# Channel shuffle in 32 equal tiles: small tiles at both ends, six buffers, copies shared by VectorE and ScalarE

## The chip, the cores and the metric

The kernel runs on one core of one Trainium2 chip. The metric is the device time of one execution in microseconds (us), lower is better. "Span" is the part of an execution that the profile's records cover; the time is 1.7 to 2.2 us longer than the span.

## The reference

```python
batch, h, w, c = 16, 64, 64, 256          # float32, groups = 8
x = x.reshape(batch, h, w, groups, channels_per_group)
x = x.transpose(0, 1, 2, 4, 3)            # swap group and channel in the group
x = x.reshape(batch, h, w, c)
```

It is a pure permutation inside each pixel of 256 channels. It computes nothing, reads 67.11 MB from HBM and writes 67.11 MB back.

## The kernel before

There are 32 tiles of 16 pixels a partition (2 MB each). A tile is loaded by SyncE's DMA queue, permuted by one copy within SBUF, on GpSimd for even tiles and on VectorE for odd ones, and stored by ScalarE's DMA queue. There are five buffers for loads and five for stores.

```python
_Q = int(os.environ.get("CS_Q", "16"))
_IN_BUFS = int(os.environ.get("CS_IN_BUFS", "5"))
_OUT_BUFS = int(os.environ.get("CS_OUT_BUFS", "5"))
_COPY_ENGINES = os.environ.get("CS_COPY_ENGINES", "gv")
# ... cut ...
    for t in range(ntiles):
        in_tile = in_pool.tile([P, free], mybir.dt.float32)
        nc.sync.dma_start(out=in_tile, in_=x_t[t])

        out_tile = out_pool.tile([P, free], mybir.dt.float32)

        src = in_tile.rearrange("p (i g j) -> p i j g", g=G, j=CPG)
        dst = out_tile.rearrange("p (i j g) -> p i j g", j=CPG, g=G)
        do_copy(copy_engines[t % len(copy_engines)], dst, src)

        nc.scalar.dma_start(out=out_t[t], in_=out_tile)
```

Of the kernel before, what the change touches and what calls it, by code (L numbers as in the profile page):

```python
# [2 lines left out]

# [4 lines left out]


_Q = int(os.environ.get("CS_Q", "16"))
_IN_BUFS = int(os.environ.get("CS_IN_BUFS", "5"))
_OUT_BUFS = int(os.environ.get("CS_OUT_BUFS", "5"))
_COPY_ENGINES = os.environ.get("CS_COPY_ENGINES", "gv")


@with_exitstack
def kernel(
    ctx: ExitStack,
    tc: tile.TileContext,  # L20
    x: bass.AP,
    groups: bass.AP,
    out: bass.AP,
):
    nc = tc.nc

    b, h, w, c = x.shape
    G = int(groups)
    CPG = c // G
    assert G * CPG == c, (c, G)  # L30

    P = nc.NUM_PARTITIONS

    n_pix = b * h * w
    assert n_pix % P == 0

    q = _Q
    pix_per_tile = P * q
    ntiles = n_pix // pix_per_tile
    assert ntiles * pix_per_tile == n_pix, (n_pix, pix_per_tile)  # L40

    free = q * c

    x_t = x.rearrange("b h w c -> (b h w c)").rearrange(
        "(t p f) -> t p f", p=P, f=free
    )
    out_t = out.rearrange("b h w c -> (b h w c)").rearrange(
        "(t p f) -> t p f", p=P, f=free
    )

    in_pool = ctx.enter_context(tc.tile_pool(name="in_pool", bufs=_IN_BUFS))
    out_pool = ctx.enter_context(tc.tile_pool(name="out_pool", bufs=_OUT_BUFS))

    eng_map = {"v": nc.vector, "g": nc.gpsimd, "s": nc.scalar}
    copy_engines = [eng_map[ch] for ch in _COPY_ENGINES]

    def do_copy(eng, dst, src):
        if eng is nc.scalar:
            eng.copy(out=dst, in_=src)
        else:  # L60
            eng.tensor_copy(out=dst, in_=src)  # L61

    for t in range(ntiles):
        in_tile = in_pool.tile([P, free], mybir.dt.float32)
        nc.sync.dma_start(out=in_tile, in_=x_t[t])  # L65

        out_tile = out_pool.tile([P, free], mybir.dt.float32)

        src = in_tile.rearrange("p (i g j) -> p i j g", g=G, j=CPG)
        dst = out_tile.rearrange("p (i j g) -> p i j g", j=CPG, g=G)  # L70
        do_copy(copy_engines[t % len(copy_engines)], dst, src)

        nc.scalar.dma_start(out=out_t[t], in_=out_tile)


# [1 line left out]
_INS = ['x', 'groups']  # L77
_OUTS = [((16, 64, 64, 256), 'float32')]
#: Inputs that are plain numbers.
_NUMBERS = {'groups': 8}  # L80


# [26 lines left out]
```

## Time and profile before

| | before |
|---|---|
| time, median (range) | 318.0 us (317.92 to 318.02) |
| span of the profiled execution | 316.3 us |
| DMA, mean over the span | 424 GB/s |
| GpSimd busy / VectorE busy | 36% / 20% |

From the profile's page: the share of time that the 16 DMA engines are busy, in 40 equal slices of the span (9 is 90% or more), what they moved in each slice, and the DMA queues (q1 and q10 carry the loads and the stores), with packets, MB and the time of their packets as a share of the 16 engines' span.

```profile
DMA  7999999999999999999999999999999999999997
GB/s 290 431 402 431 431 431 431 431 431 433 431 431 431 431 431 431 431 431 431 431 431 431 431 431 431 431 431 431 431 431 431 431 431 431 431 431 431 433 431 332
...
q1 hardware_dynamic: 4608, 67.11, 50.0%
q10 hardware_dynamic: 4608, 67.11, 49.5%
HBM read 67.11 MB, written 67.11 MB: 424 GB/s over the span
```

38 of 40 slices are at 90% or more, nearly all at 431 GB/s, and the packets of the two queues fill 99.5% of the engines' time. The copies are far from that. These are the groups of instructions: count, busy us, mean ns of one, then the idle time before them and what ended it.

```profile
L61 POOL COPY out_tile<-in_tile 128x4096 f32<-128x4096 f32 x16 | 114.5, 7157 | 182.3 <-DMA in_tile<-in_x_dram 182.3
L61 DVE COPY out_tile<-in_tile 128x4096 f32<-128x4096 f32 x16 | 63.8, 3985 | 240.0 <-DMA in_tile<-in_x_dram 240.0
```

Both engines that copy idle for most of the span, waiting for loads. Here are the busy time, DMA share and GB/s in some stretches (microseconds of the span, a packet is counted where it starts):

```profile
core 0: us, DVE busy (x) POOL busy (x), PEclk, DMA share, GB/s
2.00:4.00 2.00, 0.00 (x0) 0.00 (x0) 1.00 0.72 246
4.00:9.00 5.00, 0.00 (x0) 0.43 (x1) 1.00 1.00 426
...
30.00:290.00 260.00, 51.47 (x14) 92.44 (x13) 1.00 1.01 431
290.00:314.00 24.00, 3.89 (x1) 7.11 (x1) 1.00 1.00 430
314.00:315.00 1.00, 0.00 (x0) 0.00 (x0) 1.00 0.43 180
315.00:316.00 1.00, 0.00 (x0) 0.00 (x0) 1.00 0.00 0
...
```

The engines are full from 4 us on; 180 GB/s in the last microsecond with traffic, nothing after 315 us.

### The profile page before, as it was taken

Reading aid. Unit: us, or ns where it says so; the run is one execution under the profiler, and the core shown is the slowest. Engines: PE = TensorE matmul, PEld = TensorE weight load, DVE = VectorE, ACT = ScalarE, POOL = GpSimd, SP = SyncE. Lnnn points to the kernel's source line nnn. Section 1 sums busy time; section 2 is a strip of 40 time slices with the busy share of each in tenths; the row PEclk is TensorE's granted clock in tenths of the full one; section 3 lists DMA queues with packets and bytes.
Section 4 is the critical chain, followed back from the end, with each engine's and each line's share of the span. In section 5 each row is a group of like instructions: output and inputs, shape, how many; then the busy total and the mean of one; then the engine's idle time right before and its main releaser. Section 6 shows DMA issues by size and latency. Waiting matters only on the chain.

```text
span 316.3 us, 247 instructions
## 1 busy us (share of the span) xinstructions
DVE 63.8 (20%) x16; POOL 114.7 (36%) x20
## 2 busy tenths in 40 slices
DVE  0344004040130402204021040310404004040040
POOL 0863350803508044080530806217062260713500
DMA  7999999999999999999999999999999999999997
GB/s 290 431 402 431 431 431 431 431 431 433 431 431 431 431 431 431 431 431 431 431 431 431 431 431 431 431 431 431 431 431 431 431 431 431 431 431 431 433 431 332
DMA packets 9216, 134.22 MB, mean 424 GB/s; under 512 B 1024, under 2 KB 1024, under 8 KB 1024
## 3 DMA queue, kind: packets, MB, share of 16 engines
q1 hardware_dynamic: 4608, 67.11, 50.0%
q10 hardware_dynamic: 4608, 67.11, 49.5%
HBM read 67.11 MB, written 67.11 MB: 424 GB/s over the span
## 4 chain that ended last, share of the span: by engine, by line
DMA 94%; DVE 1%; SPq 0%; issue 0%; DVEq 0%
DMA in_tile<-in_x_dram 94%; DVE out_tile L61 1%; SPq L65 0%; DVEq L61 0%
## 5 line engine op out<-in xcount | busy, mean ns | idle before, releaser
L61 POOL COPY out_tile<-in_tile 128x4096 f32<-128x4096 f32 x16 | 114.5, 7157 | 182.3 <-DMA in_tile<-in_x_dram 182.3
L61 DVE COPY out_tile<-in_tile 128x4096 f32<-128x4096 f32 x16 | 63.8, 3985 | 240.0 <-DMA in_tile<-in_x_dram 240.0
L90 POOL MEMSET const-float32-0.0<- 128x1 f32 x1 | 0.1, 99 | 0.2 <-issue 0.2
L90 POOL MEMSET const-bfloat16-1.0<- 128x1 bf16 x1 | 0.1, 103 | 0.0
L90 POOL MEMSET const-uint8-127<- 128x1 uint8 x1 | 0.1, 103 | 0.0
L90 POOL MEMSET const-float32-1.0<- 128x1 f32 x1 | 0.1, 99 | 0.0
## 6 DMA issues: line engine op xcount, KB each, us to landing
in_tile<-in_x_dram SPq DMA_DIRECT2D x32, 2048.0 KB, 38.8
out_dram<-out_tile ACTq DMA_DIRECT2D x32, 2048.0 KB, 25.3
```

Source lines behind the costliest of these rows:

```text
L61: eng.tensor_copy(out=dst, in_=src)
L90: nc = _bacc.Bacc("TRN2", target_bir_lowering=False, num_devices=1)
```

## The change

The intent is to start storing earlier and to finish with a short tail: tiles of 4, 4 and 8 pixels a partition first and 8, 4, 4 last. Each copy is split in two halves, on VectorE and ScalarE, to shorten it, and there are six buffers instead of five. The diff, cut to its core:

```diff
-_Q = int(os.environ.get("CS_Q", "16"))
-_IN_BUFS = int(os.environ.get("CS_IN_BUFS", "5"))
-_OUT_BUFS = int(os.environ.get("CS_OUT_BUFS", "5"))
-_COPY_ENGINES = os.environ.get("CS_COPY_ENGINES", "gv")
+_SIZES = [4, 4, 8] + [16] * 30 + [8, 4, 4]
+_IN_BUFS = 6
+_OUT_BUFS = 6
+_SHARES = (("vector", 1), ("scalar", 1))
 # ... cut ...
-    for t in range(ntiles):
-        in_tile = in_pool.tile([P, free], mybir.dt.float32)
-        nc.sync.dma_start(out=in_tile, in_=x_t[t])
 # ... cut ...
-        do_copy(copy_engines[t % len(copy_engines)], dst, src)
-        nc.scalar.dma_start(out=out_t[t], in_=out_tile)
+    for q in _SIZES:
+        in_tile = in_pool.tile([P, biggest * c], F32, name="in_tile")
+        nc.sync.dma_start(out=in_tile[:, : q * c], in_=rows(x_flat, first, q))
+        out_tile = out_pool.tile([P, biggest * c], F32, name="out_tile")
+        at, total = 0, sum(n for _, n in _SHARES)
+        for k, (engine, n) in enumerate(_SHARES):
 # ... cut: upto = end of this engine's share of the q pixels ...
+                permute(engine, out_tile[:, cols], in_tile[:, cols])
+        nc.scalar.dma_start(out=rows(out_flat, first, q), in_=out_tile[:, : q * c])
+        first += P * q
```

More of the change, by code (lines that the diff above doesn't have):

```diff
@@ L2 @@
-import os
 from contextlib import ExitStack
@@ L8 @@
 from concourse._compat import with_exitstack
-_Q = int(os.environ.get("CS_Q", "16"))
-_IN_BUFS = int(os.environ.get("CS_IN_BUFS", "5"))
-_OUT_BUFS = int(os.environ.get("CS_OUT_BUFS", "5"))
-_COPY_ENGINES = os.environ.get("CS_COPY_ENGINES", "gv")
+F32 = mybir.dt.float32
+P = 128
+_SIZES = [4, 4, 8] + [16] * 30 + [8, 4, 4]
+_IN_BUFS = 6
+_OUT_BUFS = 6
+_SHARES = (("vector", 1), ("scalar", 1))
 @with_exitstack
@@ L29 @@
     CPG = c // G
-    assert G * CPG == c, (c, G)
-    P = nc.NUM_PARTITIONS
-    n_pix = b * h * w
-    assert n_pix % P == 0
-    q = _Q
-    pix_per_tile = P * q
-    ntiles = n_pix // pix_per_tile
-    assert ntiles * pix_per_tile == n_pix, (n_pix, pix_per_tile)
-    free = q * c
-    x_t = x.rearrange("b h w c -> (b h w c)").rearrange(
-        "(t p f) -> t p f", p=P, f=free
-    )
-    out_t = out.rearrange("b h w c -> (b h w c)").rearrange(
-        "(t p f) -> t p f", p=P, f=free
-    )
+    assert G * CPG == c
@@ L51 @@
+    assert sum(_SIZES) * P == b * h * w
+    biggest = max(_SIZES)
+    x_flat = x.rearrange("b h w c -> (b h w c)")
+    out_flat = out.rearrange("b h w c -> (b h w c)")
     in_pool = ctx.enter_context(tc.tile_pool(name="in_pool", bufs=_IN_BUFS))
     out_pool = ctx.enter_context(tc.tile_pool(name="out_pool", bufs=_OUT_BUFS))
-    eng_map = {"v": nc.vector, "g": nc.gpsimd, "s": nc.scalar}
-    copy_engines = [eng_map[ch] for ch in _COPY_ENGINES]
-    def do_copy(eng, dst, src):
-        if eng is nc.scalar:
-            eng.copy(out=dst, in_=src)
-        else:
-            eng.tensor_copy(out=dst, in_=src)
@@ L63, with rows @@
-    for t in range(ntiles):
-        in_tile = in_pool.tile([P, free], mybir.dt.float32)
-        nc.sync.dma_start(out=in_tile, in_=x_t[t])
-        out_tile = out_pool.tile([P, free], mybir.dt.float32)
-        src = in_tile.rearrange("p (i g j) -> p i j g", g=G, j=CPG)
-        dst = out_tile.rearrange("p (i j g) -> p i j g", j=CPG, g=G)
-        do_copy(copy_engines[t % len(copy_engines)], dst, src)
-        nc.scalar.dma_start(out=out_t[t], in_=out_tile)
+    def rows(flat, first, q):
+        return flat[first * c : (first + P * q) * c].rearrange("(p f) -> p f", p=P)
@@ new lines, in permute @@
+    def permute(engine, dst, src):
+        src = src.rearrange("p (i g j) -> p i j g", g=G, j=CPG)
+        dst = dst.rearrange("p (i j g) -> p i j g", j=CPG, g=G)
+        if engine == "scalar":
+            nc.scalar.copy(out=dst, in_=src)
+        else:
+            getattr(nc, engine).tensor_copy(out=dst, in_=src)
+    first = 0
+    for q in _SIZES:
[4 more added lines that the diff above has]
+        for k, (engine, n) in enumerate(_SHARES):
+            last = k == len(_SHARES) - 1
+            upto = q if last else min(q, at + -(-q * n // total))
+            if upto > at:
+                cols = slice(at * c, upto * c)
+                permute(engine, out_tile[:, cols], in_tile[:, cols])
+            at = upto
+        nc.scalar.dma_start(out=rows(out_flat, first, q), in_=out_tile[:, : q * c])
+        first += P * q
```

## The prediction

> **What bounds the kernel now.** The 16 DMA engines. The page's slices show a DMA share of 90% or more and 431 GB/s in nearly all 40 slices; the first (290 GB/s) and the last (332 GB/s) are clearly lower. The chain of waits gives 94% of the 316.3 us span to loads. VectorE is busy 20%, GpSimd 36%, and in the list of waits both wait only for loads (240.0 and 182.3 us). The Trainium skill, "DMA: Bandwidth & Descriptors", section "Where 436 GB/s comes from", gives 435 GB/s as the ceiling of the 16 ports; the trace agrees with 431 to 433 in steady slices.
>
> The chain repeats every 38.84 us for four tiles in and four out: 9.71 us a tile (2.1 MB each way), 432 GB/s. All 134.22 MB at this rate take 310.7 us. Small windows show the first packets at about 1.5 us and the last at 314.5 us. So only about 5.6 us of the span is not steady transfer: 1.5 before the first packet, about 2.3 in ramp-up and where stores begin (98 to 262 GB/s at 2.5 to 3.5 us, 246 GB/s at 19 us), 1.8 for the last store to be confirmed.
>
> **What the change does.**
> - Halved copies: today 7.1 us (GpSimd) or 3.9 us (VectorE) a tile. VectorE's half is about 1.95 us (half of 3.87). ScalarE's half, 2048 elements, is estimated at 1.9 us from the Trainium skill, "ScalarE: Activation LUTs", section "What ACT_TABLE_LOAD costs" (186 ns + 0.833 ns an element). No ScalarE copy is in this trace. Copies wait for loads, not the reverse: worth 0. A table load on ScalarE, if any, precedes the first landing: 0.
> - Six buffers instead of five: loads are in flight continuously already (SyncE's queue waits 244.1 us for loads, 3.2 for copies). Worth 0.
> - Small first tiles: the first store starts at about 7 us instead of 15.7. But loads fill the DMA engines from 3.5 us on, so an earlier store only displaces load packets. Worth 0. Issues of about 0.42 us still outpace a 0.5 MB tile (1.2 us).
> - Small last tiles: the last copy ends at 303.7 us with 10.6 us of stores still queued, so its latency is hidden already. After the change stores lag loads less (I estimate 3 to 4 MB, 7 to 9 us, instead of 6 MB), still more than receipt, half copy and issue (4 to 6 us). Worth 0.
> - Added: 4 loads, 4 stores, and packets of 4 and 8 KB instead of 16 KB in 12 transfers, some 0.1 to 0.5 us; ramp-up may change by half a microsecond either way.
>
> **Prediction.** Nearly nothing changes on the critical path: 318.2 us, range 317.4 to 319.1. Faster by over 2%: 0.01; within 2%: 0.97; slower: 0.02.
>
> **What would show the steps.** 431 GB/s throughout; GpSimd idle, ScalarE and VectorE near 65 us each; first store issued at 6 to 8 us; first packet near 1.5 us, last about 1.8 us before the end. From the last load's landing to the end shrinks from 16.6 us to 7 to 11 us without the span shrinking: the loads simply end later.
>
> **What would make it wrong.** A store queue that runs dry at the end, a visible gap of DMA share in the last slice (up to 4 us, 1%); small packets that slow the engines; ScalarE copies much longer than 2 us, delaying the stores it issues; or a steady rate that depends on how loads and stores interleave, which one trace can't show.

## The result, and the profile after

| | before | after |
|---|---|---|
| time, median (range) | 318.01 us (317.92 to 318.13) | 319.16 us (318.76 to 319.61) |
| span of the profiled execution | 316.3 us | 317.5 us |
| ratio (95% interval) | 1 | 1.0036 (1.0022 to 1.005) |

A ratio here is the mean time of one kernel's fast runs over that of the other's of the same rounds, so it is not quite the ratio of the medians that are quoted. Within 2% nothing changed, as predicted. But the change is slower by 1.15 us, and that is clear of noise; the measured 319.16 us lies 0.06 us above the predicted range. What was to be explained is one microsecond in 318.

The same parts of the page:

```profile
DMA  7999999999999999999999999999999999999996
GB/s 285 401 430 427 429 431 431 431 431 431 431 431 429 436 433 429 433 431 431 429 428 429 431 429 433 431 431 431 430 429 436 431 428 433 431 431 428 420 441 281
...
q1 hardware_dynamic: 5184, 67.11, 49.8%
q10 hardware_dynamic: 5184, 67.11, 49.5%
q14 instruction: 3, 0.02, 0.0%
HBM read 67.11 MB, written 67.11 MB: 423 GB/s over the span
```

The share is still 9 nearly everywhere and the rate still about 431. Two things differ. The last slice falls from 332 to 281 GB/s, and there is a new queue, q14, that carries instructions: three packets. The copies:

```profile
L49 ACT COPY out_tile<-in_tile 128x2048 f32<-128x2048 f32 x30 | 111.0, 3708 | 171.6 <-DMA in_tile<-in_x_dram 171.6
L51 DVE COPY out_tile<-in_tile 128x2048 f32<-128x2048 f32 x30 | 62.3, 2075 | 218.9 <-DMA in_tile<-in_x_dram 218.9
```

ScalarE takes 3.71 us for half a tile, not 1.9; VectorE takes 2.08. Both still wait only for loads, as the list of waits says (engine and line, what it waited for, us in total, times, longest):

```profile
DVE out_tile L51 <- DMA in_tile<-in_x_dram: 242.1, 36, 8.3
ACT out_tile L49 <- DMA in_tile<-in_x_dram: 188.0, 33, 13.8
```

The chain of waits gives loads 81% and stores 8%. ScalarE's copies get 3%, which are single links and not an accumulated cost:

```profile
DMA in_tile<-in_x_dram 81%; DMA out_dram<-out_tile 8%; ACT out_tile L49 3%; SPq L56 1%; ACTq L66 0%
```

The stretches show where the time went:

```profile
core 0: us, DVE busy (x) ACT busy (x) POOL busy (x), PEclk, DMA share, GB/s
2.00:4.00 2.00, 0.00 (x0) 0.01 (x1) 0.00 (x0) 1.00 0.93 369
4.00:9.00 5.00, 1.50 (x3) 2.43 (x3) 0.00 (x0) 1.00 1.01 369
...
30.00:290.00 260.00, 55.28 (x28) 98.11 (x28) 0.00 (x0) 1.00 1.01 431
290.00:314.00 24.00, 3.63 (x4) 7.72 (x4) 0.00 (x0) 1.00 1.00 424
314.00:315.00 1.00, 0.00 (x0) 0.00 (x0) 0.00 (x0) 1.00 0.87 356
315.00:316.00 1.00, 0.00 (x0) 0.00 (x0) 0.00 (x0) 1.00 0.23 94
316.00:317.00 1.00, 0.00 (x0) 0.00 (x0) 0.00 (x0) 1.00 0.03 12
```

From 30 to 290 us there is no visible difference. At 4 to 9 us, though, the change moves 369 GB/s where the kernel before moves 426. From 2 to 4 us it is the other way round (369 against 246), so that over 2 to 9 us both move nearly the same, 2.58 and 2.62 MB: the mean rate shows next to no loss at the start. At the end the engines no longer stop together: traffic trickles on at 94 and 12 GB/s from 315 us, when the kernel before has ended. When the mean rate falls from 356 to 94 GB/s in one microsecond, some of the 16 engines are done and others are not. So the question is not how busy the DMA engines are on average, but which of them ends last.

### One DMA engine at a time

The trace records each packet's start and duration, but not its engine. In the steady stretch that can be recovered: an engine starts a 16 KB packet every 607 ns, so the starts form 16 chains, one for each engine, and each has to carry 512 such packets' worth of bytes. Chains that start close to each other are easily confused, above all in the last 30 us of the change, where packets of 4, 8 and 16 KB mix. A second rule keeps them apart: on each queue, every transfer puts eight data packets of equal size and then one of 4 bytes on each engine (each queue has 576 packets of 4 bytes for the 36 transfers of the change). Following the chains from 35 us after the first packet to the end gives, for each engine, the end of its last packet and how much it had lost by 35 us against back-to-back packets. A slip is a packet that starts late against its chain. Times here count from the first packet (1.76 us of the span before, 1.77 after). The last five engines of each kernel, worked out in this way from the packet records:

```
                 before                         after
          end us   lost by 35 us        end us   lost by 35 us   slips after 35 us
last      313.35   2.20                 314.60   2.42            305 + 533 ns, at instruction packet 2
          313.14   1.99                 314.43   2.54            306 + 244 ns, at instruction packet 1
          313.02   1.87                 313.97   1.56            306 + 424 ns, at instruction packet 3
          313.02   1.86                 313.92   2.58            none
          313.01   1.85                 313.85   2.52            none
```

Not every packet can be given to one chain with certainty. Every assignment from 150 us on that was found to fit both rules well has the same two engines last. The third line is uncertain: another chain lies so close that the 424 ns, or this end, may be its own, and the line's numbers leave some 0.3 us of its end unexplained.

The last packet ends 1.25 us later (314.60 against 313.35), and the spans differ by 1.24 us. Of this, 0.84 us are the two slips beside the second instruction packet, and 0.22 us is what the last engine lost more in the first 35 us (2.42 against 2.20). The other 0.19 us came later: 0.56 us lost from 35 us to the end, without the slips, instead of 0.37, for the extra small packets and completions (4 KB packets start every 155 ns, a quarter of 607 would be 152). The average engine explains much less than that: the mean of all 16 ends is 0.46 us later. Five engines had lost 2.42 to 2.58 us by 35 us, the others at most 1.92. Two of the five also carried an instruction packet, and these two end last; two that carried none end 0.50 and 0.57 us after the last engine of the kernel before. So two costs met on the same engines here, and there they add.

In the first microseconds the mean number of DMA engines that are busy, in steps of 0.5 us of the span, from the same records (overlapping packets counted as 16 at most):

```
span us from       3.0   3.5   4.0   4.5   5.0   5.5   6.0   6.5   7.0   7.5
before            15.7  16.0  16.0  16.0  16.0  16.0  16.0  16.0  16.0  16.0
after             16.0  16.0  16.0  13.4  15.3  16.0  16.0  16.0  15.4  14.1
```

At 4.5 us, once the two first loads of 0.5 MB are through and the third load should follow, engines stand idle: 4 of the 16 at 4.8 us, and all are busy again at 5.3 us, so no engine loses more than about 0.6 us here. No store has begun at that time (the first packet of a store starts at 9.5 us). There is a second, shorter dip from 7.4 to 7.8 us. It is likely, but not shown, that the five engines which had lost most by 35 us are the ones that stood idle here.

Here are the DMA queues in the stretch from 158 to 161 us of the span, where one of the instruction packets falls:

```profile
q10 hardware_dynamic: 42, 0.69, 53.5%
q1 hardware_dynamic: 37, 0.61, 47.6%
q14 instruction: 1, 0.01, 0.6%
```

It takes 309 ns on one engine. The chain of that engine slips by 306 ns at this very point, and 0.85 us later by another 244 ns, for which the records have no packet. At the other two packets the slips are 305 and 533 ns, and 306 and 424 ns (the last one perhaps on another chain). The packets come about 3 to 5 us after the 64th recorded instruction of ScalarE, the 64th of VectorE, and the 79th of SyncE. The kernel before ends with 67 recorded instructions on ScalarE, 47 on VectorE and 71 on SyncE, and has no such packet in its span. The Trainium skill, "Runtime: NRT & Kernel Launch", section "Instruction fetch mechanics", says that a sequencer fetches the next block of its program over a DMA queue of its own while it executes the current one, in blocks of 16 KiB, and calls the cost "mostly hidden". The trace agrees so far that no wait of a compute engine is put down to these packets. But it shows a packet of 8 KB, and the DMA engine that carries it falls behind.

### The profile page after: what moved, and what is told of

It is laid out like the page before. It is cut to its first block, busy times and chain, and to the rows that moved or that the text cites. A ratio compares the mean times of both kernels' runs of the same rounds, so it can differ in the third digit from the quotient of the medians.

```text
span 317.5 us, 339 instructions
## 1 busy us (share of the span) xinstructions
DVE 67.2 (21%) x36; ACT 120.8 (38%) x37; POOL 0.2 (0%) x4
## 4 chain that ended last, share of the span: by engine, by line
DMA 88%; another core or an unknown queue 5%; ACT 3%; SPq 1%; issue 0%; ACTq 0%
DMA in_tile<-in_x_dram 81%; DMA out_dram<-out_tile 8%; ACT out_tile L49 3%; SPq L56 1%; ACTq L66 0%
## 5 line engine op out<-in xcount | busy, mean ns | idle before, releaser
L49 ACT COPY out_tile<-in_tile 128x2048 f32<-128x2048 f32 (+2 forms) x36 | 119.5, 3326 | 188.1 <-DMA in_tile<-in_x_dram 188.0
L51 DVE COPY out_tile<-in_tile 128x2048 f32<-128x2048 f32 (+2 forms) x36 | 67.2, 1868 | 242.1 <-DMA in_tile<-in_x_dram 242.1
```

Of the source, the lines that this page charges most:

```text
L49: nc.scalar.copy(out=dst, in_=src)
L51: getattr(nc, engine).tensor_copy(out=dst, in_=src)
```

## The experiments

My theory is this. The end is set by the slowest of 16 saturated DMA engines. The change loses on single engines, (1) at the small first loads, because the next load's packets are not there when a small one is through, and (2) at instruction packets, which come with more instructions.

The rivals are: (A) the halved copies or ScalarE's late issue of stores; (B) the small last tiles, which let the engines end apart; (C) instruction packets are harmless; (D) the early small stores disturb the loads.

All twelve runs gave correct results. "Span" is the median of a run's five executions; "last packet" and "after it" (the time from the last packet to the end of the span) are of the profiled one, and so is "beyond" (the time minus the span).

| run | time us (range) | ratio to before (95%) | span | last packet at | after it | beyond |
|---|---|---|---|---|---|---|
| before | 318.04 (317.93 to 318.37) | | 316.3 | 315.11 | 1.16 | 1.73 |
| the change | 319.16 (318.76 to 319.61) | 1.0036 (1.0022 to 1.005) | 317.4 | 316.37 | 1.14 | 1.79 |
| even tiles | 318.96 (318.67 to 319.11) | 1.0026 (1.0013 to 1.0039) | 317.2 | 315.53 | 1.66 | 1.77 |
| no small first | 319.08 (319.01 to 319.2) | 1.0031 (1.0019 to 1.0044) | 317.3 | 315.46 | 1.79 | 1.79 |
| no small last | 319.11 (318.92 to 319.64) | 1.0038 (1.0024 to 1.0051) | 317.3 | 315.97 | 1.37 | 1.77 |
| small tiles alone | 319.46 (318.97 to 319.98) | 1.0045 (1.0032 to 1.0058) | 317.3 | 315.88 | 1.37 | 2.19 |
| spare instructions | 318.52 (318.43 to 318.93) | 1.0018 (1.0005 to 1.003) | 316.7 | 315.54 | 1.16 | 1.77 |
| many spare instructions | 350.19 (348.03 to 350.58) | 1.1006 (1.0991 to 1.1021) | 348.4 | | | |
| small tiles, 2nd load on other queue | 318.70 (318.6 to 318.8) | 1.0019 (1.0007 to 1.0032) | 316.5 | 315.19 | 1.23 | 2.18 |
| small last alone | 318.63 (318.28 to 319.17) | 1.0017 (1.0005 to 1.003) | 316.6 | 315.57 | 1.43 | 2.17 |
| copies in quarters | 318.32 (318.14 to 318.51) | 1.0009 (0.9996 to 1.0021) | 316.5 | 315.58 | 1.17 | 1.76 |
| the change, 2nd load on other queue | 318.71 (318.65 to 318.86) | 1.0022 (1.001 to 1.0035) | 316.9 | 315.60 | 1.29 | 1.77 |
| six buffers alone | 318.12 (317.97 to 318.33) | 1.0004 (0.999 to 1.0018) | 316.3 | 315.02 | 1.16 | 1.79 |
| the change again | 318.96 (318.81 to 319.45) | 1.0034 (1.0021 to 1.0046) | 317.2 | 315.75 | 1.29 | 1.77 |

The row "before" takes its time from the nine executions beside the first four experiments, the rest from the profile before. Beside the other two groups of four it measured 318.04 and 318.08 us. The change's own ratio and its repetition are from two sessions. The first four experiments, the next four and the last four ran on three different chips, each group beside the kernel before.

From the packet records of the profiled executions, the engine that ended last in each run (us after the first packet; where chains could not be followed from 35 us, the loss is by a later time, which adds up to 0.1 us):

| run | last engine ends | lost by 35 us | slips at an instruction packet |
|---|---|---|---|
| before | 313.35 | 2.20 | |
| the change | 314.60 | 2.42 | 305 + 533 ns |
| even tiles | 313.81 | 1.82 | 306 + 531 ns |
| no small first | 313.74 | 1.57 | 306 + 531 ns |
| no small last | 314.24 | 3.08 | |
| small tiles alone | 314.15 | 2.82 | |
| small tiles, 2nd load on other queue | 313.42 | 2.20 (by 120 us) | |
| small last alone | 313.81 | 2.48 | |
| copies in quarters | 313.84 | 1.84 | 306 + 530 ns |
| the change, 2nd load on other queue | 313.87 | 1.70 (by 80 us) | 306 + 406 ns |
| six buffers alone | 313.26 | 2.11 | |
| the change again | 314.02 | 1.63 (by 50 us) | 306 + 409 ns |

Some loss at the start is always there, and it varies: without small first tiles the worst engine of one of these runs (not always the one that ended last) lost 2.07 to 2.48 us by 35 us, with them and one load queue 2.31 to 3.08 us.

### Undoing one part of the change (three runs) and doing the tiles alone (one run)

Even tiles:

```diff
-_SIZES = [4, 4, 8] + [16] * 30 + [8, 4, 4]
+_SIZES = [16] * 32
```

> The change with all 32 tiles of 16 pixels (halved copies and six buffers stay). Theory: the slowest of the 16 DMA engines sets the end; the change loses on single engines, about 1.0 to 1.4 us at the small first loads (load queue dry between small tiles) and about 0.6 to 0.8 us on one engine for each of three instruction-fetch packets that the trace shows in mid-run. So this run loses only the fetches: 318.4 to 318.8 us. Rival A, the halved copies and ScalarE's later issue of stores cost the time: as the changed kernel, 319.0 to 319.4. Rival B, the small last tiles cost it: as before, 318.0.

No small first tiles:

```diff
-_SIZES = [4, 4, 8] + [16] * 30 + [8, 4, 4]
+_SIZES = [16] * 31 + [8, 4, 4]
```

> The change without its small first tiles (31 tiles of 16, then 8, 4, 4). Theory: the loss at the first loads goes, the fetches and a little packet overhead (0.1 to 0.2 us) stay: 318.5 to 319.0 us. Rival B (small last tiles let the engines end apart): no gain, 319.0 to 319.4.

No small last tiles:

```diff
-_SIZES = [4, 4, 8] + [16] * 30 + [8, 4, 4]
+_SIZES = [4, 4, 8] + [16] * 31
```

> The change without its small last tiles (4, 4, 8, then 31 tiles of 16). Theory: the first loads still run dry, so 318.9 to 319.3 us, and the last slice is as ragged as with the whole change. Rival B: 318.0 to 318.4 us and all engines end together.

Small tiles alone, in the changed kernel's code:

```diff
-_IN_BUFS = 6
-_OUT_BUFS = 6
-_SHARES = (("vector", 1), ("scalar", 1))
+_IN_BUFS = 5
+_OUT_BUFS = 5
+_WHOLE = ("gpsimd", "vector")
 # in the loop, in place of the two halves:
+        permute(_WHOLE[t % 2], out_tile[:, : q * c], in_tile[:, : q * c])
```

> The kernel before (whole copies in turn on GpSimd and VectorE, five buffers) with the small tiles first and last. Theory: the loss at the first loads is there without halved copies: 318.6 to 319.2 us, fewer instruction-fetch packets in the span. Rival A (halved copies, ScalarE): 318.0 to 318.3 us.

Read by times alone these four say nothing sensible: small tiles alone cost all of the loss (+1.4 us), all the rest without small tiles costs most of it (+0.9), and taking away either end's small tiles wins nothing. The costs don't add over the runs. That is how a maximum over engines behaves: take away what delays the last engine, and the next one is nearly as late.

The traces tell them apart. Small tiles alone has no instruction packet in its span, and its four last engines (314.00 to 314.15 us after the first packet) are those that lost 2.67 to 2.82 us by 35 us, against 2.20 us at most before. Only 11.1 and 12.1 of 16 engines are busy at 4.5 and 5.0 us of the span. Even tiles is full there. Its last engine had lost only 1.82 us by 35 us, but it carried the second instruction packet (slips of 306 and 531 ns) and ended at 313.81. With no small last tiles, the last engine, at 314.24, lost 3.08 us by 35 us and carried no packet; those with the second and the third packet come next, at 313.73 and 313.70.

Rival A falls as the whole cause, since small tiles alone loses more without any ScalarE copy. But even tiles shows that the halved copies (with six buffers, which alone cost nothing, see below) do cost 0.9 us; in its trace the engine that ends last is one that carries an instruction packet, not one that waits for a late store. Rival B falls too: without small last tiles the loss is as large as with them. My numbers for even tiles (up to 318.8) and for small tiles alone (up to 319.2) were 0.2 and 0.3 us too low; no small first tiles (up to 319.0) came out 0.1 us too high for my range, inside the range that I had given to rival B. The last columns of the first table show what I had not counted. In even tiles the span ends 1.66 us after the last packet (1.14 to 1.43 in the runs with no packet there), and a third instruction packet falls in just that time; from 316 to 317.2 us the DMA queues hold nothing else:

```profile
q14 instruction: 1, 0.01, 2.4%
```

No small first tiles has 1.79 us there, also with a packet at 316.88 us. In the three runs whose "beyond" is 2.17 us or more, an instruction packet comes after the end of the span; in all the other runs there is none there, and "beyond" is 1.79 us at most. That looks like a cost of 0.2 to 0.6 us for a fetch at the very end. It is read from the traces' coincidence only; no run here changed it by itself.

### Instructions without any change of transfers (three runs)

```diff
+        for _ in range(2):                      # 14 in the second run
+            nc.vector.memset(spare[0], 0.0)
+            nc.gpsimd.memset(spare[1], 0.0)
         nc.scalar.dma_start(out=out_t[t], in_=out_tile)
```

> The kernel before with two tiny memsets a tile more on VectorE and on GpSimd (their results are never used); no transfer changes. In the traces so far a packet of 8 KB of the instruction queue appears in mid-run just after ScalarE's and VectorE's 64th recorded instruction, and the one DMA engine that carries it ends 0.55 to 0.85 us later than it would. Theory: VectorE (47 recorded instructions before) and GpSimd (56) now pass 64, so two instruction packets in mid-run, two DMA engines late, 318.2 to 318.9 us depending on which engines carry them. Rival C (the DMA engines end apart because of the copies' or the stores' timing, instruction packets are harmless): two packets, but 317.9 to 318.1 us as before.

> As the run before, with 14 spare memsets a tile on VectorE and on GpSimd, some 500 recorded instructions on each. Theory: about four instruction packets for each of the two, eight in all, some on the same DMA engine: 318.6 to 319.8 us. Rival C: 317.9 to 318.2 us.

The first gave 318.52 us, in the predicted range, but the test was not clean. The spare memsets depend on nothing, so all of them were placed at the start of both engines' programs, as the timeline shows (start, us, engine, line):

```profile
0.73 10.29 POOL L78 MEMSET spare<- 128x8 f32 x64 [0.29 <-POOLq L97]
0.81 8.46 DVE L77 MEMSET spare<- 128x8 f32 x64 [0.81 <-PEq L97]
10.96 7.13 POOL L61 COPY out_tile<-in_tile 128x4096 f32<-128x4096 f32 x1
```

So the first copy started at 11.0 us instead of 8.6, and the two packets came at 10.7 and 12.4 us, not in mid-run. They followed the 66th instruction of VectorE and about the 70th of GpSimd.

The second was a bad experiment, and its 350 us say nothing about fetches. On GpSimd the spare memsets are 153 ns long and 0.48 us apart in the timeline, so 14 of them take some 7 us a tile, and the copies fell behind. The group, and the waits that came of it:

```profile
L78 POOL MEMSET spare<- 128x8 f32 x448 | 68.4, 153 | 25.8 <-POOLq L97 0.3
```

```profile
DVE out_tile L61 <- DMA out_dram<-out_tile: 156.6, 10, 16.9
POOL out_tile L61 <- DMA out_dram<-out_tile: 110.5, 9, 15.2
DVE out_tile L61 <- POOL spare L78: 30.0, 3, 16.0
```

VectorE waited 30.0 us for GpSimd's memsets, and both waited for stores, which had come in bursts. The eight instruction packets of the page are as expected, but their cost is lost in this.

The third run does it properly, with the same copies on the same engines in four pieces each:

```diff
-        do_copy(copy_engines[t % len(copy_engines)], dst, src)
+        for k in range(4):
+            px = slice(k * q // 4, (k + 1) * q // 4)
+            do_copy(copy_engines[t % len(copy_engines)],
+                    out_tile...[:, px]..., in_tile...[:, px]...)
```

> The kernel before with each copy issued as four copies of 4 pixels on the same engine: no transfer, no buffer and no engine changes, only more instructions (some 95 to 110 recorded on VectorE and on GpSimd, in place of 47 and 56). This does in mid-run what the spare memsets did only at the start. Theory: two instruction packets of 8 KB in mid-run, just after VectorE's and GpSimd's 64th recorded instruction; the DMA engines that carry them lose 0.55 to 0.85 us each: span 316.5 to 317.2, 318.2 to 318.9 us. Rival C (the packets are harmless): 317.9 to 318.1 us.

The groups and the instruction queue of its page:

```profile
L61 POOL COPY out_tile<-in_tile 128x1024 f32<-128x1024 f32 x64 | 122.2, 1953 | 174.4 <-DMA in_tile<-in_x_dram 174.4
L61 DVE COPY out_tile<-in_tile 128x1024 f32<-128x1024 f32 x64 | 68.6, 1145 | 234.7 <-DMA in_tile<-in_x_dram 234.7
```

```profile
q14 instruction: 2, 0.02, 0.0%
```

Two packets, at 215.2 and 226.0 us of the span, the first after GpSimd's 71st recorded instruction and the second after VectorE's 67th. The chains slip by 306 and 306 ns at once, and by 212 and 530 ns about 1 us later. The engine that ended last (313.84 us after the first packet) is the one with 306 + 530 ns; it had lost only 1.84 us by 35 us. So the packets are not harmless to the engine that carries them. But the time moved by only 0.24 us, and the interval of the ratio (0.9996 to 1.0021) includes no change at all. What a fetch costs the kernel is its slip less the lead that its engine happened to have. Rival C falls for single engines; for the whole time, this run leaves the size open between nothing and about half a microsecond.

### The gap after the small first loads (three runs)

```diff
+        loader = nc.scalar if t == 1 else nc.sync
-        nc.sync.dma_start(out=in_tile[:, : q * c], in_=rows(x_flat, first, q))
+        loader.dma_start(out=in_tile[:, : q * c], in_=rows(x_flat, first, q))
```

This was done to the kernel with small tiles alone, and then (with `first == 4 * P` for `t == 1`) to the whole change, beside the change unedited.

> The small tiles alone (whole copies, five buffers), but the second load is issued by ScalarE's queue. Theory: at 2.5 to 2.9 us after the first packet some DMA engines stand idle 0.9 to 1.7 us because the third load's descriptors have not reached them when two tiles of 4 pixels are done; with the second load on the other queue the third is next in its queue 1.2 us earlier, so these gaps shrink or vanish: 318.2 to 318.8 us (small tiles alone: 319.46). Rival D (early small stores disturb the loads): no change, 319.2 to 319.8.

> The whole change, with its second load issued by ScalarE's queue. Theory: no DMA engine stands idle for over 0.8 us at 2.5 to 2.9 us after the first packet, so the two engines that ended last in the changed kernel no longer do; those that carry the three instruction packets end last instead: 318.4 to 318.9 us, 0.3 to 0.7 us under the change on the same chip. Rival D (the early small stores disturb the loads): as the change, within 0.2 us.

> The changed kernel unedited, once more on the chip of the other three runs, for comparison: 318.8 to 319.6 us, three instruction packets in mid-run at about 159, 225 and 255 us of the span, and one or more DMA engines idle over 0.8 us near 2.7 us after the first packet.

The stretch from 4 to 9 us (busy time of the engines that copy, then DMA share and GB/s), for small tiles alone and then with its second load on the other queue:

```profile
4.00:9.00 5.00, 1.59 (x1) 1.85 (x1) 1.00 1.00 349
```

```profile
4.00:9.00 5.00, 2.65 (x1) 2.84 (x2) 1.00 1.05 444
```

and for the change again and then the change with its second load on the other queue:

```profile
4.00:9.00 5.00, 1.65 (x3) 2.58 (x3) 0.00 (x0) 1.00 0.99 384
```

```profile
4.00:9.00 5.00, 2.16 (x3) 3.04 (x3) 0.00 (x0) 1.00 1.07 437
```

349 GB/s became 444, and 384 became 437. The number of busy DMA engines from the packet records:

```
span us from                               4.0   4.5   5.0   5.5   6.0
small tiles alone                         16.0  11.1  12.1  14.4  16.0
  with the 2nd load on the other queue    16.0  16.0  16.0  16.0  16.0
the change again                          16.0  13.4   9.4  13.3  16.0
  with the 2nd load on the other queue    16.0  16.0  16.0  16.0  16.0
```

The gap is gone in both. From 2 to 4 us both kernels with the second load on the other queue move less than their partners (313 against 369 and 309 against 356 GB/s), so the gain over the whole start is smaller than these stretches suggest. Rival D can't explain the gap, because the first packet of a store starts only at 9.6 us (small tiles alone) and 8.9 us (the change again). The times don't decide about D: with the edit the first store was also issued later (at 8.3 instead of 5.9 us, and at 6.5 instead of 5.4 us). For small tiles alone the median span went from 317.3 to 316.5 us, 0.2 above before; the rest of its 318.70 us is the 0.4 us beyond the span. The change improved from 318.96 to 318.71 us on the same chip, 0.25 by the medians (0.3 to 0.7 expected), and the ranges of the two overlap only between 318.81 and 318.86 us. I had expected the engines with instruction packets to end last there. They do: the last three (313.87, 313.84 and 313.67 us) are those of the three packets, and had lost only 1.70 to 1.84 us by 80 us. But in the profiled execution of the change again the last two engines, at 314.02 and 313.98 us, also carry instruction packets, and those that had lost most at the start (2.31 and 2.30 us by 50 us) end at 313.62 and 313.61. Where the gap doesn't set the end, closing it wins little.

So it is shown that this edit closes the gap, and that small tiles alone gain by it (318.97 to 319.98 us without it, 318.6 to 318.8 with it, though on another chip); for the change the gain is small, and the intervals of the two ratios overlap. Why the third load's packets come late is not shown: the trace has the issue of the third load at 1.6 us of the span, long before 4.5 us, and nothing in between. The edit also moves that issue 0.47 us forward (to 1.16 us), and no run separates this from the other queue.

### Small last tiles alone, and six buffers alone

```diff
 # small tiles alone, with
-_SIZES = [4, 4, 8] + [16] * 30 + [8, 4, 4]
+_SIZES = [16] * 31 + [8, 4, 4]
```

> The kernel before with the small tiles at the end only (31 tiles of 16, then 8, 4, 4), whole copies, five buffers. Theory: no dry first loads and no instruction packets in mid-run, only some more packets: 318.0 to 318.4 us. Rival B (small last tiles cost the time): 318.8 to 319.4.

```diff
 # the kernel before, with
-"CS_IN_BUFS", "5"   "CS_OUT_BUFS", "5"
+"CS_IN_BUFS", "6"   "CS_OUT_BUFS", "6"
```

> The kernel before with six buffers of each kind, nothing else. Every theory here: no effect, 317.9 to 318.2 us, no instruction packet in the span.

Small last tiles alone took 318.63 us, 0.2 above my range. Its median span is 0.3 us above before, and its profiled execution has the fetch after the end (2.17 us beyond). They win nothing, as there was nothing to win: the stores were queued up behind each other anyway. Six buffers alone are at 318.12 us, no difference. Their DMA packets are those of the kernel before, 9216, without an instruction packet:

```profile
DMA packets 9216, 134.22 MB, mean 425 GB/s; under 512 B 1024, under 2 KB 1024, under 8 KB 1024
```

No run came out below the kernel before. It is close to what its own steady rate allows: 134.22 MB at 432 GB/s are 310.7 us, and of the remaining 5.6 us of the span, 1.8 pass before the first packet and 1.2 after the last.

## Why the prediction was right or wrong

- **The bound was right.** The DMA engines limit the kernel before and after, at 431 GB/s. The Trainium skill's ceiling of 435 GB/s ("DMA: Bandwidth & Descriptors", section "Where 436 GB/s comes from") was not passed by any steady stretch.
- **Halved copies, "worth 0", was one of the two steps that failed, and the larger term in the profiled execution.** "Copies wait for loads, not the reverse" was right. But with equal tiles, halved copies and six buffers took 318.96 us, and six buffers alone 318.12. What the prediction's sum lacks is the instructions of the change themselves: its line "Added" counts loads, stores and smaller packets, and no fetch of instructions. In the change's profiled execution the two slips beside one instruction packet are 0.84 of the 1.25 us by which the last packet is late. That the fetches make the whole 0.9 us is read from the traces; the run that added instructions alone (copies in quarters) moved the time by 0.24 us, with an interval that includes none.
- **The size of ScalarE's half was wrong, without effect.** It is 3.71 us where the estimate from the Trainium skill ("ScalarE: Activation LUTs", section "What ACT_TABLE_LOAD costs", 186 ns + 0.833 ns an element) gave 1.9 us, so ScalarE is busy 120.8 us, not 65. From the forms with 512 and 2048 elements (1108 and 3708 ns) this copy takes 1.69 ns an element. It had room enough for the error not to matter.
- **Six buffers worth 0: right**, by a run of their own.
- **Small last tiles, "worth 0": nearly right.** The stores did not run dry; the time from the last load's landing (308.6 us) to the end is 8.9 us, within the predicted 7 to 11. The extra packets cost the last engine 0.19 us after 35 us, within the predicted 0.1 to 0.5. By themselves they took 318.63 us, 0.6 more than before; 0.4 of that stand beyond the span.
- **Small first tiles, "worth 0", because "issues of about 0.42 us still outpace a 0.5 MB tile (1.2 us)", is the other step that failed.** The issue instructions do outpace it, but the packets of the third load were not at the engines when the second was through. Engines stood idle for about 0.6 us in the change, 1.1 in its repetition and 1.3 with small tiles alone. By 35 us the worst engine of the change had lost 2.58 us, against 2.20 before, and the one that ended last 0.22 us more than the last one before. Small tiles alone took 319.46 us, and 318.70 with the second load on the other queue, which filled the gap.
- **The method failed along with it.** I costed the loss by mean rates. The 16 engines end on average 0.46 us later, which added to 318.0 us is inside the range; but the kernel ends with its last engine, 1.25 us later. No sentence of the prediction asked which engine that would be.
- **There was chance in the size.** In the first profiled execution (319.30 us) the costs of both failed steps met on the same engines; in that of the repetition (318.81 us) they did not, and the last packet was 0.67 us later than before instead of 1.25. Whether this explains the spread of the change's times (318.76 to 319.61 us) is not shown: the other executions have no trace.

## What to carry to other kernels

When DMA is saturated from end to end, the time is that of the slowest DMA engine: look at how sharply the traffic stops, not only at the mean rate, and expect small costs on different engines to combine as a maximum, so that undoing one of them may win nothing, and costs on the same engine to add up. Small first loads on a single queue can leave engines idle where one large load would not; if they are needed, try the second on the other queue and check the busy engines of the first 10 us. Splitting copies that nobody waits for only adds instructions, and their fetches run on the same DMA engines as the data.

## What the Trainium skill lacked or had wrong

- "Runtime: NRT & Kernel Launch", section "Instruction fetch mechanics", calls the cost of a block fetch "mostly hidden". It lacks what the fetch costs the DMA engine that carries it beside a saturated stream: an 8 KB packet of 309 ns, with a slip of that engine's packets by 305 to 306 ns and another of 212 to 533 ns about 1 us later on that engine (in two traces perhaps on another). The first such packet came near an engine's 64th to 71st recorded instruction (79th to 80th on SyncE), if the engine that reached such a count just before is the one that fetched. This is no rule: before the change ScalarE reaches 67 without a packet, and with small tiles and the second load on the other queue one comes at 311.6 us, at ScalarE's 73rd and SyncE's 70th.
- No page says what a fetch at the end of the program costs: runs with one there have 0.2 to 0.6 us more between the last packet and the end of the execution (coincidence in the traces, not tested).
- "DMA: Bandwidth & Descriptors" gives rates and a fixed cost by transfer size. It lacks that consecutive 0.5 MB loads on one queue can leave engines idle (for about 0.6 to 1.7 us here) although the next load was issued 3 us earlier, and that the second load on the other queue closes the gap (349 to 444 GB/s at 4 to 9 us). Its section "Issuing engines are not separate DMA queues" says that issuing from several engines only saves the sequencer's issue time. Here it saved 0.47 us of issue time for the third load, and gaps of up to 1.3 us were gone; whether the other queue or the earlier issue did this is not separated.
- "ScalarE: Activation LUTs", section "What ACT_TABLE_LOAD costs": the formula gives 1.9 us for 2048 elements a lane, and the section doesn't say that it is for sources without steps. This float32 copy, whose source steps by 32 elements, took 3.71 us; no run here has a copy without steps, so the cause of the difference is not shown.
